# Output projection of a gated-attention layer: the first two token tiles interleaved, and the scaled rows kept in the weight rows' buffers

## The chip, the cores and the metric

The kernel runs on one core of a Trainium2 chip. The time is device microseconds (us) of one execution. TensorE (PE) multiplies matrices, VectorE (DVE), ScalarE (ACT) and GpSimd (POOL) work element by element, SyncE (SP) issues the DMAs. Every engine works through its own list of instructions in order and waits on semaphores.

## The reference, cut to what matters

One layer of a diffusion transformer, float32, 1024 tokens of width 1024. A gated linear attention `o_gla` (4 heads of 128) and a short row convolution `o_sc` (512 channels) stand side by side, and go through the output projection `w_out`:

```
o_gla = rmsnorm(o_f + o_b, g_head).reshape(bsz, t, GLA_WIDTH) * jax.nn.silu(og)
o_sc  = sb * dwconv_row(sc * sx, w_sc, b_sc, rows, width)
yx    = concatenate([o_gla, o_sc], axis=-1)
x     = x + gt1 * rmsnorm(yx @ w_out[i], g_post_mix[i])
hx    = modulate(rmsnorm(x, g_pre_ffn[i]), sh2, sc2)
x     = x + gt2 * rmsnorm(conv_ffn(hx, ...), g_post_ffn[i])
```

In the sum `yx @ w_out` the rows 512 to 1023 of `w_out` meet `o_sc`, which needs no gate any more (the *ungated half*); the rows 0 to 511 meet `o_gla`, which is first multiplied by `silu(og)` (the *gated half*).

## The kernel before

A float32 product is made of three matmuls (`mm3`, L144 to L146): each operand is split into a high part and a rest (`split`: ACT makes the high part at L127, DVE the rest at L134), and high x high, high x rest and rest x high are added in one PSUM bank. Tokens are tiled by 128, so there are 8 token tiles c = 0 to 7.

The order on PE is that in which the code is written. On ACT, DVE, POOL and SP a scheduler sets the order at build time, until token tile 7; from there on ACT, DVE and POOL keep the written order too, and SP alone is scheduled.

Names. `pw` is a memory pool that holds the first weight rows' split (`woh`, `wol` without number) and three buffers with the tag `wor` for raw rows of `w_out`; it is closed after the projection, and the pool `pc` of the next stage takes its place (raw rows `wr` of the up-projection, `u`, `rs`). `wp` holds `wraw`, `whi`, `wlo` in two buffers each. `ps_mm` has 4 PSUM banks. `scd` and `ogd` are spilled in DRAM: the convolution's results and the gate's arguments.

Tile c of the projection goes through these helpers (cut):

```
worder = (4, 5, 6, 7, 0, 1, 2, 3)

def mix_prep(c):                         # operands of tile c
    mh, ml = wp.tile(... "whi"), wp.tile(... "wlo")
    SY.dma_start(so, sc_d[c // 4][c % 4])
    split(so, mh[:, 4:8, :], ml[:, 4:8, :])          # ungated half
    SY.dma_start(sog, og_d[c // 4][c % 4])           # sog: 2 buffers
    SY.dma_start(xt, ap["x"][c * P : (c + 1) * P, :])
    PE.transpose(pt[...], on[c][...], ident)  x4     # L1031
    act(sf, sf, AF.Silu)                             # sf is sog
    V.scalar_tensor_tensor(sf, pt, col("ghead"), sf, ALU.mult, ALU.mult)   # L1034
    split(sog, mh[:, 0:4, :], ml[:, 0:4, :])         # gated half
def w_out(mh, ml, py, nhs, ns):          # mm3 per n in ns and half nh, contraction tile worder[n]
def half_stats(py, nh, xn, ss):          # ACT: sum of squares of a bank; DVE: xn = bank * gv1
def residual(c, xt, xn, ss, fill):       # POOL: rstd; DVE L1056: xt += xn * r; SP: x1_d[c] <- xt;
                                         # ACT: squares of xt into xn; POOL: rstd; DVE L1067: xn = xt * r
def norm_tiles():                        # L1075
    return p2.tile([P, D], F32, tag="xn", bufs=1, ...), cp.tile([P, 2], F32, tag="ss2", bufs=2, ...)
def norm2(c, xn, dg):                    # PE: 8 transposes of xn (L1086); ACT: 8 rows blk <- ps
```

So of the eight contraction steps n of a tile, n = 0 to 3 are ungated and n = 4 to 7 gated. A tile is 48 matmuls (8 steps, 2 halves of the output, 3 matmuls each). The loop calls `w_out` for tile 0 with n 0 to 3 of both halves, `mix_prep(1)`, then n 4 to 7, then `half_stats` of both halves and `residual`. For tiles 1 to 6: half 0 with all n, `mix_prep(c + 1)`, half 1 with n 0 to 4, `norm2(c - 1)`, `half_stats` of half 0, n 5 to 7, `half_stats` of half 1, `residual`. Tile 7 has its own order, in which the first up-projections are prepared too (`early_prep(p)`: a raw row `wr` is loaded, L1131, and split, L127 and L1181; tiles `p`). After the projection `early_dot(0)` to `early_dot(3)` and the products with the sums `mx` of `blk` follow on PE. The sums of weight rows `rs` (POOL, L1155) come from `wr` too.

Of the kernel before, what the change touches and what calls it, by code (L numbers as in the profile page):

```python
# [8 lines left out]
F32 = mybir.dt.float32  # L9
# [10 lines left out]
D = 1024  # L20
CT = 256
P = 128
KT = D // P
NT = T // P
# [94 lines left out]
def build(nc, ap, out, dbg=None):  # L119
# [3 lines left out]
    def nm(s="t"):  # L123
        return f"{s}{next(names)}"

    def act(o, i, fn=AF.Copy, **kw):
        return S.activation(o, i, fn, **kw)  # L127

    def split(raw, hi, lo, eng=None, heng=None):
        if heng is None:  # L130
            act(hi, raw)
        else:
            heng.tensor_copy(hi, raw)
        (eng or V).tensor_tensor(lo, raw, hi.bitcast(F32), ALU.subtract)  # L134
# [13 lines left out]
    with tile.TileContext(nc) as tc, tc.manual_schedule(engines={mybir.EngineType.PE}):  # L148
        pools = {}

        def popen(name, side=None, **kw):
            cm = tc.tile_pool(name=name, side=side, **kw)
            pools[name] = (cm, cm.__enter__())
            return pools[name][1]
# [9 lines left out]
        cp = popen("cp", "left", bufs=1)  # L164
# [4 lines left out]
        ps_mm, ps_at, ps_ms = "mm", "at", "ms"  # L169
# [4 lines left out]
        def bank(n):  # L174
            return pools[n][1].tile([P, 512], F32, tag=n, name=nm("ps"))
# [7 lines left out]
        def col(name, j=0, n=1):  # L183
            o, w = COLS[name]
            return cols[:, o + j : o + j + n]
# [806 lines left out]
        p2 = popen("p2", "right", bufs=1, reuse_waits="tile")  # L992
# [26 lines left out]
        def mix_prep(c):  # L1019
            mh = wp.tile([P, KT, P], F32R, tag="whi", name=nm("mh"))  # L1020
            ml = wp.tile([P, KT, P], F32R, tag="wlo", name=nm("ml"))
            so = pvo.tile([P, H, P], F32, tag="vo", name=nm("so"))
            SY.dma_start(so, sc_d[c // 4][c % 4])
            split(so, mh[:, 4:8, :], ml[:, 4:8, :])
            sog = p2.tile([P, H, P], F32, tag="sog", bufs=2, name=nm("sog"))
            SY.dma_start(sog, og_d[c // 4][c % 4])
            xt = p2.tile([P, D], F32, tag="x", bufs=2, name=nm("x"))
            SY.dma_start(xt, ap["x"][c * P : (c + 1) * P, :])
            pt = bank(ps_ms)
            for h in range(H):  # L1030
                PE.transpose(pt[:, h * P : (h + 1) * P], on[c][:, h * DV : (h + 1) * DV], ident)  # L1031
            sf = sog.rearrange("p h t -> p (h t)")
            act(sf, sf, AF.Silu)
            V.scalar_tensor_tensor(sf, pt, col("ghead"), sf, ALU.mult, ALU.mult)  # L1034
            split(sog, mh[:, 0:4, :], ml[:, 0:4, :])
            return mh, ml, xt

        def w_out(mh, ml, py, nhs, ns):
            for n in ns:
                kt = worder[n]  # L1040
                for nh in nhs:
                    s = slice(nh * 512, nh * 512 + 512)
                    mm3(py[nh], (mh[:, kt, :], ml[:, kt, :]), (woh[kt][:, s], wol[kt][:, s]), n == 0, n == KT - 1)

        def half_stats(py, nh, xn, ss):
            s = slice(nh * 512, nh * 512 + 512)
            act(xn[:, s], py[nh], AF.Square, scale=1.0 / 32, accum_out=ss[:, nh : nh + 1])
            V.tensor_tensor(xn[:, s], py[nh], gv1[:, s], ALU.mult)

        def residual(c, xt, xn, ss, fill):  # L1050
            r = cp.tile([P, 4], F32, tag="rstd", bufs=6, name=nm("rstd"))
            G.tensor_scalar(r[:, 0:1], ss[:, 0:1], ss[:, 1:2], EPS, ALU.add, ALU.add)
            G.tensor_tensor(r[:, 0:1], r[:, 0:1], mhalf[:, 0:1], ALU.pow)
            for f in fill[:1]:
                f()
            V.scalar_tensor_tensor(xt, xn, r[:, 0:1], xt, ALU.mult, ALU.add)  # L1056
            SY.dma_start(x1_d[c], xt)
            dump(f"x1_{c}", xt, [P, D])
            ss = cp.tile([P, 1], F32, tag="ss", bufs=4, name=nm("ss"))
            act(xn, xt, AF.Square, accum_out=ss)  # L1060
            r = rstd(ss, 1, 1.0 / D)
            for f in fill[1:3]:
                f()
            if c < NT - 1:
                for f in fill[3:]:
                    f()
                V.tensor_scalar(xn, xt, r[:, 0:1], None, ALU.mult)  # L1067
                return xn, None
            dg = p2.tile([P, P], F32, name="dg2")
            V.tensor_scalar(dg, ident, r[:, 0:1], None, ALU.mult)  # L1070
            for f in fill[3:]:
                f()
            return xt, dg

        def norm_tiles():  # L1075
            return p2.tile([P, D], F32, tag="xn", bufs=1, name=nm("xn")), cp.tile([P, 2], F32, tag="ss2", bufs=2, name=nm("ss2"))

        def norm2(c, xn, dg):
            cs = slice((c % 4) * P, (c % 4 + 1) * P)
            th = c // 4  # L1080
            for g in range(2):
                pt = bank(ps_at)
                for j in range(4):
                    o, i = pt[:, j * P : (j + 1) * P], xn[:, (4 * g + j) * P : (4 * g + j + 1) * P]
                    if dg is None:
                        PE.transpose(o, i, ident)  # L1086
                    else:
                        PE.matmul(o, i, dg, start=True, stop=True)
                for j in range(4):
                    ft = 4 * g + j  # L1090
                    act(blk[g][th][:, j, cs], pt[:, j * P : (j + 1) * P], AF.Identity,
                        bias=sh2[:, ft : ft + 1], scale=a2[:, ft : ft + 1])
            x11, x12, x21, x22 = (blk[g][h][:, :, cs] for g in range(2) for h in range(2))
            if th == 0:
                split(x11, b11[0][:, :, cs], b11[1][:, :, cs], heng=V)
                split(x21, b21[0][:, :, cs], b21[1][:, :, cs])
            else:
                d = t7[:, :, cs]
                return [lambda: V.tensor_tensor(d, x22, x12, ALU.subtract),
                        lambda: V.tensor_tensor(x12, x12, x11, ALU.subtract),  # L1100
                        lambda: V.tensor_tensor(x11, x11, d, ALU.add),
                        lambda: V.tensor_tensor(x21, x21, x11, ALU.subtract)]
# [81 lines left out]

        c2, c6, c1 = slice(0, 2 * P), slice(2 * P, 3 * P), slice(3 * P, 4 * P)
        gv1 = p2.tile([P, D], F32, name="gv1")
        mix = mix_prep(0)
        SY.dma_start(gv1, rows(16, "gp1"))
        gv2_row = rows(40, "gp2")
        normed = None  # L1190
        for c in range(NT):
            py = [bank(ps_mm) for _ in range(2)]
            mh, ml, xt = mix
            last, sums = normed, []
            if c == NT - 1:
                ordered = tc.manual_schedule(
                    engines={mybir.EngineType.Activation, mybir.EngineType.DVE, mybir.EngineType.Pool})
                ordered.__enter__()
            if c == 0:
                w_out(mh, ml, py, (0, 1), range(4))  # L1200
                mix = mix_prep(1)
                w_out(mh, ml, py, (0, 1), range(4, 8))
                xn, ss = norm_tiles()
                half_stats(py, 0, xn, ss)
            elif c == NT - 1:
                w_out(mh, ml, py, (0, 1), range(5))
                early_prep(0)()
                sums = norm2(c - 1, *last)
                mixed(6, c2)
                mixed(7, c2)  # L1210
                w_out(mh, ml, py, (0, 1), range(5, 6))
                w_out(mh, ml, py, (0,), range(6, 8))
                xn, ss = norm_tiles()
                half_stats(py, 0, xn, ss)
                w_out(mh, ml, py, (1,), range(6, 8))
            else:
                w_out(mh, ml, py, (0,), range(8))
                mix = mix_prep(c + 1)
                w_out(mh, ml, py, (1,), range(5))
                sums = norm2(c - 1, *last) or []  # L1220
                xn, ss = norm_tiles()
                half_stats(py, 0, xn, ss)
                w_out(mh, ml, py, (1,), range(5, 8))
            half_stats(py, 1, xn, ss)
            if c == NT - 1:
                sums.insert(1, early_prep(1))
            normed = residual(c, xt, xn, ss, sums)
# [156 lines left out]
        py = popen("py", "left", bufs=1)  # L1384
# [239 lines left out]
```

## Time and profile before

| what | value |
|---|---|
| median of 3 runs | 1183.76 us (1183.09 to 1184.44) |
| the profiled execution | 1187.9 us, of which the span from the first to the last instruction is 1186.1 us |
| mean granted clock of TensorE | 0.988 of full speed |
| busy share: PE, DVE, ACT, POOL | 97%, 74%, 44%, 40% |
| the output projection on PE | 427 to 533 us of the span |

PE is busy nearly throughout, so what matters are the places where it waits or runs at a lower clock. The table of PE's waits, the timeline of each engine, and the table of windows (with the granted clock) tell these.

### The profile page before, as it was taken

What the parts mean: (1) busy time and instruction counts of PE and PEld (TensorE: products, weight loads), DVE (VectorE), ACT (ScalarE), POOL (GpSimd) and SP (SyncE); (2) the same over time, 40 slices, a digit from 0 to 9 for tenths busy, and PEclk for the clock granted to TensorE, in tenths of its full rate; (3) what the DMA queues carried; (4) which work ended last, traced back from release to release, by engine and by line L of the source; (5) the groups of instructions that cost most, each with busy time, mean ns of one, the idle gap of its engine ahead of it and who ended that gap; (6) DMA issues with size and microseconds to landing.
All of it is one profiled execution on the core that took longest, in us unless ns stands there. A gap on an engine that the chain in (4) does not pass through costs nothing. (4 is left out here: it accounts for less than half of the span.)

```text
span 1186.1 us, 15908 instructions
## 1 busy us (share of the span) xinstructions
PE 1150.9 (97%) x5770; PEld 946.1 (80%) x5770; DVE 878.3 (74%) x1215; ACT 518.5 (44%) x931; POOL 479.0 (40%) x467
## 2 busy tenths in 40 slices
PE   8899999999999979999999999999999999999997
PEld 6689967877887868888787788888888888888885
DVE  4965547898769445559688987878787887777676
ACT  5745155643234145556343333333434254544453
POOL 3111001334355201114877776877686871000002
PEclk9999999999999989999999999999999999999999
DMA  9884854311102163232233442233223259978672
GB/s 347 269 293 136 266 153 134 121 57 46 54 18 75 60 217 129 107 125 71 76 101 100 134 141 71 90 125 116 85 79 125 95 161 326 361 246 278 215 241 98
DMA packets 80128, 176.19 MB, mean 149 GB/s; under 512 B 9809, under 2 KB 21585, under 8 KB 80050
## 3 DMA queue, kind: packets, MB, share of 16 engines
q1 hardware_dynamic: 80050, 175.19, 44.4%
q8 instruction: 45, 0.74, 0.3%
q14 instruction: 33, 0.27, 0.1%
HBM read 142.38 MB, written 32.78 MB: 148 GB/s over the span
## 5 line engine op out<-in xcount | busy, mean ns | idle before, releaser
L1296 DVE SCALAR_TENSOR_TENSOR y<-u,cols,y 128x945 f32<-128x945 f32 (+2 forms) x176 | 214.8, 1222 | 3.7 <-ACT y L127 1.3
L144 PE MATMUL ps<-mx,p 128*128 128x512 f32 x440 | 173.6, 395 | 2.9 <-ACT p L127 1.7
L145 PE MATMUL ps<-mx,p 128*128 128x512 f32 x440 | 173.0, 393 | 0.0
L146 PE MATMUL ps<-mx,p 128*128 128x512 f32 x440 | 172.7, 392 | 0.0
L134 POOL TENSOR_TENSOR p<-rs,p 128x512 fp32r<-128x512 f32 x88 | 116.3, 1326 | 88.8 <-ACT p L127 85.0
L146 PE MATMUL ps<-p,p 128*128 128x512 f32 x308 | 120.1, 390 | 0.2
L145 PE MATMUL ps<-p,p 128*128 128x512 f32 x308 | 120.0, 389 | 0.0
L144 PE MATMUL ps<-p,p 128*128 128x512 f32 x308 | 119.9, 389 | 0.0
L634 POOL TENSOR_TENSOR wl<-wr,wh 128x256 fp32r<-128x256 f32 x64 | 52.7, 854 | 159.3 <-ACT wh L127 159.2
L144 PE MATMUL ps<-hxh,wh 128*128 128x512 f32 x256 | 107.5, 420 | 0.0
L229 DVE CUSTOM_DVE_ANT_0 ada<-ada,cb 128x1024 f32<-128x1024 f32 x64 | 79.9, 1263 | 34.2 <-DMA ada<-in_ada 34.1
L144 PEld LDWEIGHTS ps<-mx,p 128*128 128x128 f32 x440 | 82.6, 188 | 25.8 <-ACT u L127 5.0
L146 PE MATMUL ps<-hxh,wl 128*128 128x512 f32 x256 | 101.4, 396 | 0.0
L145 PE MATMUL ps<-hxl,wh 128*128 128x512 f32 x256 | 101.0, 394 | 0.0
L146 PEld LDWEIGHTS ps<-mx,p 128*128 128x128 f32 x440 | 82.6, 188 | 18.6
L127 ACT ACTIVATE p<-rs 128x512 fp32r<-128x512 f32 x88 | 54.5, 622 | 98.0 <-POOL rs L1155 98.0
L145 PEld LDWEIGHTS ps<-mx,p 128*128 128x128 f32 x440 | 82.6, 188 | 18.3
L134 POOL TENSOR_TENSOR p<-wr,p 128x512 fp32r<-128x512 f32 x58 | 76.2, 1314 | 13.1 <-ACT p L127 13.1
L127 ACT ACTIVATE y<-u,cols 128x1024 f32<-128x1024 f32 x22 | 26.6, 1210 | 106.1 <-DVE u L1358 106.1
L144 PE MATMUL ps<-b,p 128*128 128x512 f32 x176 | 69.6, 396 | 0.0
L145 PE MATMUL ps<-b,p 128*128 128x512 f32 x176 | 69.4, 395 | 0.0
L146 PE MATMUL ps<-b,p 128*128 128x512 f32 x176 | 69.4, 394 | 0.0
(271 smaller groups left out, 2636.0 us busy)
## 6 DMA issues: line engine op xcount, KB each, us to landing
ada<-in_ada SPq DMA_DIRECT2D x64, 512.0 KB, 4.6
wr<-in_wu SPq DMA_DIRECT2D x48, 512.0 KB, 4.0
h<-hd SPq DMA_DIRECT2D x77, 256.0 KB, 4.3
hd<-h SPq DMA_DIRECT2D x73, 256.0 KB, 2.1
wdr<-in_wd SPq DMA_DIRECT2D x55, 256.0 KB, 4.0
wdr<-in_wd SPq DMA_DIRECT2D x22, 512.0 KB, 6.1
x<-in_x SPq DMA_DIRECT2D x16, 512.0 KB, 5.5
wr<-in_wb SPq DMA_DIRECT2D x16, 512.0 KB, 3.7
```

What stands on the lines that cost most here:

```text
L127: return S.activation(o, i, fn, **kw)
L134: (eng or V).tensor_tensor(lo, raw, hi.bitcast(F32), ALU.subtract)
L144: PE.matmul(ps, lh, rh, start=first, stop=False, skip_group_check=more)
L145: PE.matmul(ps, lh, rl, start=False, stop=False, skip_group_check=more)
L146: PE.matmul(ps, ll, rh, start=False, stop=last, skip_group_check=more)
L229: V.tensor_tensor_reduce(raw, raw, cbs[which], 1.0, 0.0, ALU.mult, ALU.add, dst)
L634: eng.tensor_tensor(lo[:, k : k + 2], raw[:, k : k + 2], hi[:, k : k + 2].bitcast(F32), ALU.subtract)
L1296: V.scalar_tensor_tensor(y3[:, ro, co], u3[:, ri, ci], col("wcf", 9 * p + 3 * (dr_ + 1) + dc + 1), y3[:, ro, co], ALU.mult, ALU.add)
```

## The change

Tiles 0 and 1 are prepared together ahead of the loop. PE works through the ungated half of tile 0, the ungated half of tile 1, the gated half of tile 0, the gated half of tile 1, in all four banks of `ps_mm`. `norm2(0)` moves from tile 1 to tile 2, behind 18 matmuls of its first half. In tiles 2 to 6 `half_stats` of half 0 is called ahead of `mix_prep(c + 1)`, instead of behind `norm2(c - 1)`. The scaled rows `xn` no longer have one buffer of their own in `p2`: they take the three `wor` buffers of `pw`. No operation is added or removed.

```
@@ norm_tiles
-            return p2.tile([P, D], F32, tag="xn", bufs=1, name=nm("xn")), cp.tile(...)
+            return pools["pw"][1].tile([P, D], F32, tag="wor", bufs=3, name=nm("xn")), cp.tile(...)
@@ before the loop
-        mix = mix_prep(0)
+        firsts = [mix_prep(0), mix_prep(1)]
         SY.dma_start(gv1, rows(16, "gp1"))
         gv2_row = rows(40, "gp2")
-        normed = None
-        for c in range(NT):
+        pys = [[bank(ps_mm) for _ in range(2)] for c in range(2)]
+        for c in range(2):
+            w_out(*firsts[c][:2], pys[c], (0, 1), range(4))
+        for c in range(2):
+            w_out(*firsts[c][:2], pys[c], (0, 1), range(4, 8))
+            xn, ss = norm_tiles()
+            for nh in range(2):
+                half_stats(pys[c], nh, xn, ss)
+            if c == 0:
+                mix = mix_prep(2)
+            firsts[c] = residual(c, firsts[c][2], xn, ss, [])
+        normed = firsts[1]
+        for c in range(2, NT):
@@ in the loop
-            if c == 0:
-                w_out(mh, ml, py, (0, 1), range(4))
-                mix = mix_prep(1)
-                w_out(mh, ml, py, (0, 1), range(4, 8))
-                xn, ss = norm_tiles()
-                half_stats(py, 0, xn, ss)
@@ tiles up to 6
-                w_out(mh, ml, py, (0,), range(8))
+                w_out(mh, ml, py, (0,), range(6))
+                if c == 2:
+                    norm2(0, *firsts[0])
+                w_out(mh, ml, py, (0,), range(6, 8))
+                xn, ss = norm_tiles()
+                half_stats(py, 0, xn, ss)
                 mix = mix_prep(c + 1)
                 w_out(mh, ml, py, (1,), range(5))
                 sums = norm2(c - 1, *last) or []
-                xn, ss = norm_tiles()
-                half_stats(py, 0, xn, ss)
                 w_out(mh, ml, py, (1,), range(5, 8))
```

What the scheduler makes of it stands in the order of the instructions. The first place is the start of the projection. On PE, before, at the end of tile 0's ungated half (`ps_3985` and `ps_3986` are tile 0's banks, `on` the attention output of the tile, `woh_3932` the first weight row of the gated half):

```order
L144 MATMUL ps_3986<-woh_3926,mh_3955 128x512
L145 MATMUL ps_3986<-wol_3927,mh_3955 128x512
L146 MATMUL ps_3986<-woh_3926,ml_3956 128x512
L1031 MATMUL ps_4021<-ident,on_3046 128x128 x4
L144 MATMUL ps_3985<-woh_3932,mh_3955 128x512
L145 MATMUL ps_3985<-wol_3933,mh_3955 128x512
L146 MATMUL ps_3985<-woh_3932,ml_3956 128x512
```

And with the change at the same point (tile 0 has the banks `ps_4004` and `ps_4005` now, tile 1 `ps_4006` and `ps_4007`):

```order
L144 MATMUL ps_4005<-woh_3926,mh_3955 128x512
L145 MATMUL ps_4005<-wol_3927,mh_3955 128x512
L146 MATMUL ps_4005<-woh_3926,ml_3956 128x512
L144 MATMUL ps_4006<-woh,mh_3974 128x512
L145 MATMUL ps_4006<-wol,mh_3974 128x512
L146 MATMUL ps_4006<-woh,ml_3975 128x512
```

The four transposes of tile 1 have gone ahead of all of this, and 24 matmuls of tile 1 stand between the ungated and the gated half of tile 0. On ACT, at the same place, before (`so` are the ungated operands, `sog` the gated ones; `mh_3955` is tile 0's operand, `mh_4011` tile 1's):

```order
L127 ACTIVATE mh_4011<-so_4013 128x512
L127 ACTIVATE woh_3948<-wor_3950 128x1024
L127 ACT_TABLE_LOAD
L127 ACTIVATE sog_3961<-sog_3961 128x512
L127 ACTIVATE mh_3955<-sog_3961 128x512
L127 ACTIVATE sog_4017<-sog_4017 128x512
L127 ACTIVATE mh_4011<-sog_4017 128x512
```

With the change:

```order
L127 ACTIVATE mh_3974<-so_3976 128x512
L127 ACTIVATE woh_3948<-wor_3950 128x1024
L127 ACT_TABLE_LOAD
L127 ACTIVATE sog_3961<-sog_3961 128x512
L127 ACTIVATE sog_3980<-sog_3980 128x512
L127 ACTIVATE mh_3955<-sog_3961 128x512
L127 ACTIVATE mh_3974<-sog_3980 128x512
```

The silu of tile 1 (`sog_3980`) has moved ahead of the high part of tile 0's gated operand.

The second place is SP's list of loads for the start of the projection. Before:

```order
L1023 DMA so_4099<-scd_1666 128x512
L1131 DMA wr_4753<-in_wu 128x1024
L1026 DMA sog_3961<-ogd_1664 128x512
L1028 DMA x_3963<-in_x 128x1024
L1188 DMA gv_3954<-row_3974 128x1024
L1026 DMA sog_4017<-ogd_1664 128x512
L1028 DMA x_4019<-in_x 128x1024
L1023 DMA so_4207<-scd_1666 128x512
```

With the change:

```order
L1023 DMA so_4088<-scd_1666 128x512
L1023 DMA so_4211<-scd_1666 128x512
L1131 DMA wr_4753<-in_wu 128x1024
L1026 DMA sog_3961<-ogd_1664 128x512
L1028 DMA x_3963<-in_x 128x1024
L1026 DMA sog_3980<-ogd_1664 128x512
L1028 DMA x_3982<-in_x 128x1024
L1189 DMA gv_3954<-row_3993 128x1024
```

The load of tile 3's ungated operand has moved from the end to ahead of both gated loads, and `gv` from between them to behind them.

The third place is SP at the end of the projection, where the raw weight rows of the next stage are loaded into `pc` (`wr_4933` and `wr_5019`, for `early_prep(2)` and `early_prep(3)`). Before:

```order
L1028 DMA x_4645<-in_x 128x1024
L1131 DMA wr_4933<-in_wu 128x1024
L1131 DMA wr_5019<-in_wu 128x1024
L1057 DMA x1d_1674<-x_4537 128x1024
L1131 DMA wr_5041<-in_wu 128x1024
L1057 DMA x1d_1675<-x_4645 128x1024
L1131 DMA wr_5042<-in_wu 128x1024
```

With the change:

```order
L1028 DMA x_4649<-in_x 128x1024
L1057 DMA x1d_1674<-x_4541 128x1024
L1131 DMA wr_5041<-in_wu 128x1024
L1057 DMA x1d_1675<-x_4649 128x1024
L1131 DMA wr_4933<-in_wu 128x1024
L1131 DMA wr_5019<-in_wu 128x1024
L1131 DMA wr_5042<-in_wu 128x1024
```

Both loads have moved behind the store of tile 7's rows. Ahead of `wr_4933` SP now waits for ACT as well, since `pc` lies where `pw` was, and the last user of `pw` is no longer a matmul of tile 7 but ACT's squares of tile 7's rows, which are written into `xn`.

More of the change, by code (lines that the diff above doesn't have):

```diff
@@ L1075, in norm_tiles @@
         def norm_tiles():
-            return p2.tile([P, D], F32, tag="xn", bufs=1, name=nm("xn")), cp.tile([P, 2], F32, tag="ss2", bufs=2, name=nm("ss2"))
+            return pools["pw"][1].tile([P, D], F32, tag="wor", bufs=3, name=nm("xn")), cp.tile([P, 2], F32, tag="ss2", bufs=2, name=nm("ss2"))
         def norm2(c, xn, dg):
@@ L1198, in build @@
                 ordered.__enter__()
-            if c == 0:
-                w_out(mh, ml, py, (0, 1), range(4))
-                mix = mix_prep(1)
-                w_out(mh, ml, py, (0, 1), range(4, 8))
-                xn, ss = norm_tiles()
-                half_stats(py, 0, xn, ss)
-            elif c == NT - 1:
+            if c == NT - 1:
                 w_out(mh, ml, py, (0, 1), range(5))
```

## The prediction

> **What bounds the kernel now.** I read the page's busy shares first, then the table of PE's waits, then the timeline of each engine around the two longest of these waits that the change touches.
>
> ```profile
> PE 1150.9 (97%) x5770; PEld 946.1 (80%) x5770; DVE 878.3 (74%) x1215; ACT 518.5 (44%) x931; POOL 479.0 (40%) x467
> ...
> PE ps L144 <- ACT mh L127: 6.5, 1, 6.5
> ...
> PE ps L144 <- ACT p L127: 1.7, 1, 1.7
> ...
> PE ps L1086 <- DVE xn L1067: 0.7, 1, 0.7
> ```
>
> PE sets the time: it is busy 97% of the span. Its longest wait of all is one wait of 6.5 us for `mh`, the high part of the projection's left operand. The waits of 1.7 and 0.7 us lie at the end of the projection and behind it. The reader is to see that only these three can be won or lost here; the number of matmuls stays the same. PE's timeline at the first of them:
>
> ```profile
> 426.71 0.60 PE L1031 MATMUL ps<-ident,on 128*128 128x128 f32 x4
> 427.07 0.48 PE L144 MATMUL ps<-woh,mh 128*128 128x512 f32 x1
> ...
> 432.63 0.60 PE L1031 MATMUL ps<-ident,on 128*128 128x128 f32 x4
> ...
> 439.76 0.80 PE L144 MATMUL ps<-woh,mh 128*128 128x512 f32 x1 [6.53 <-ACT mh L127]
> ...
> 443.43 0.39 PE L144 MATMUL ps<-woh,mh 128*128 128x512 f32 x1
> ```
>
> From 427.07 to 432.63 lie the 24 ungated matmuls of tile 0, 0.232 us each. Four transposes take 0.36 us (426.71 to 427.07), so the gated half could start at 432.99; it starts at 439.76, 6.77 us late. And from 439.76 to 443.43 only 9 matmuls start, in 3.67 us instead of 2.09: another 1.58 us. Why, the table of windows tells (time, then busy us and instructions of PE, PEld, DVE, ACT, POOL, granted clock, DMA share, GB/s):
>
> ```profile
> 435.00:436.00 1.00, 0.00 (x0) 0.00 (x0) 0.00 (x0) 0.00 (x0) 0.00 (x0) 1.00 1.13 379
> 436.00:437.00 1.00, 0.00 (x0) 0.00 (x0) 0.00 (x0) 0.67 (x1) 0.00 (x0) 0.61 0.91 318
> 437.00:438.00 1.00, 0.00 (x0) 0.00 (x0) 0.00 (x0) 0.99 (x2) 0.00 (x0) 0.50 1.05 424
> 442.00:443.00 1.00, 1.00 (x4) 0.76 (x3) 0.51 (x1) 0.00 (x0) 0.00 (x0) 0.50 0.89 334
> 443.00:444.00 1.00, 1.00 (x6) 0.83 (x5) 0.00 (x0) 0.52 (x1) 0.00 (x0) 0.97 0.93 301
> ```
>
> At 436.2 (0.61 of that microsecond), 3.0 us after PE fell idle at 433.23, the granted clock fell to one half, and it stayed there till 443. In all the place costs 6.77 + 1.58 = 8.35 us. Who is late there, ACT and DVE tell:
>
> ```profile
> 428.86 0.61 ACT L127 ACTIVATE mh<-so 128x512 fp32r<-128x512 f32 x1
> 430.13 0.69 DVE L134 TENSOR_TENSOR ml<-so,mh 128x512 fp32r<-128x512 f32 x1
> 436.33 1.28 ACT L127 ACT_TABLE_LOAD   x1 [4.00 <-DMA sog<-ogd]
> 437.63 0.63 ACT L127 ACTIVATE sog<-sog 128x512 f32<-128x512 f32 x1
> 438.29 0.75 DVE L1034 SCALAR_TENSOR_TENSOR sog<-ps,cols,sog 128x512 f32<-128x512 f32 x1 [4.71 <-ACT sog L127]
> 439.08 0.63 ACT L127 ACTIVATE mh<-sog 128x512 fp32r<-128x512 f32 x1 [0.82 <-DVE sog L1034]
> 439.74 0.69 DVE L134 TENSOR_TENSOR ml<-sog,mh 128x512 fp32r<-128x512 f32 x1 [0.69 <-ACT mh L127]
> ```
>
> The chain is: gate's arguments land (436.33), table load, silu, product, high part (done at 439.71). The ungated operands of tile 1 are long there: `mh` at 429.47, `ml` at 430.82.
>
> **The interleaving.** Eight transposes instead of four, then 48 ungated matmuls: PE starts them at 427.07 + 0.36 = 427.43 and has 48 x 0.232 = 11.12 us of work, to 438.55. Tile 1's operands (430.82) are wanted at 433.0, so nothing waits between. What is wanted at 438.55 is tile 0's gated operand. Two things move it: the queue of loads and ACT's order.
>
> ```profile
> 429.05 0.44 SPq L1026 DMA_DIRECT2D sog<-ogd  x1
> ...
> 430.48 0.71 SPq L1026 DMA_DIRECT2D sog<-ogd  x1
> ...
> DMA to landing us min/median/max: 9.2/9.2/9.2
> ```
>
> Tile 0's load, issued at 429.05, landed at 436.33; tile 1's, issued at 430.48, took 9.2 us, to 439.7. The DMAs are full (374 GB/s over the three windows from 435 to 438), so the order of the bytes decides. A further 256 KB load stands ahead of both now: 0.70 us, and tile 0's lands at 437.0. Between the two there is no `gv` any more, only `x` (512 KB): tile 1's lands 768 KB, 2.1 us, later, at 439.1 (at the latest as before, 439.7). Table load and silu take 436.33 to 438.29, 1.96 us: silu 0 ends at 439.0. ACT now does silu 1 next, which waits for 439.1 (439.7) and ends at 439.75 (440.35); then the high part, 0.65: PE can start at 440.4 (441.0). DVE makes both products (the second till 440.5, at the latest 441.1), then the rest part (0.7, till 441.2): the third matmul would be due 0.6 us behind the first, so it waits some 0.15 more. PE loses 1.85 to 2.45 plus 0.15; I take the middle, 2.3 us. The clock should stay full: PE was granted the full clock for 3.0 us of its idle time above.
>
> [...]
>
> So this place gives 8.35 - 2.3 = 6.05 us. Bounds: with both loads landing so early that only the old chain counts (439.76), 1.2 us are lost and 7.15 won; with the late landing 5.75.
>
> **What moves around it**, at nothing: `norm2(0)` stands 42 matmuls (9.7 us) behind tile 0's last matmul now, `norm2(1)` 39 and twelve transposes behind tile 1's. The chain between (squares, rstd, sum, squares, rstd, scaling) takes under 7.2 us, as tile 6 shows below; without those 2.5 us of cover each microsecond would be PE's. Silu 2 and 3 now stand ahead of tile 0's squares on ACT and may hold them for half a microsecond; the same cover takes it.
>
> **The squares of half 0 earlier, three buffers for `xn`.** Tile 6 is the one with a short cover:
>
> ```profile
> 520.97 0.64 ACT L127 ACTIVATE xn<-ps 128x512 f32<-128x512 f32 x1
> ...
> 521.54 0.64 ACT L127 ACTIVATE xn<-ps 128x512 f32<-128x512 f32 x1
> ...
> 528.17 1.09 PE L1086 MATMUL ps<-ident,xn 128*128 128x128 f32 x8 [0.68 <-DVE xn L1067]
> ```
>
> Both squares stand behind each other when PE is done. With the change the first is made long before, so the second starts at 520.97, 0.57 us sooner, and the chain to 528.17 with it. I take 0.55 of the 0.68 us (bounds 0 and 0.68). In tiles 2 to 5 PE doesn't wait here, so it is worth nothing there.
>
> **The price: raw rows later.** `wr_4933` and `wr_5019` were loaded at 522.08; now they wait for ACT's squares of tile 7.
>
> ```profile
> 522.08 0.82 SPq L1131 DMA_DIRECT2D wr<-in_wu  x2
> ...
> 538.81 0.18 ACT L127 ACTIVATION_READ_ACCUMULATOR xn<-x 128x1 f32 x1
> 539.04 0.33 SPq L1131 DMA_DIRECT2D wr<-in_wu  x1
> ...
> DMA to landing us min/median/max: 3.5/3.5/3.5
> ...
> 542.49 1.14 ACT L127 ACTIVATE p<-wr 128x512 fp32r<-128x512 f32 x2
> 542.96 1.47 POOL L1155 TENSOR_TENSOR rs<-wr,wr 128x512 f32<-128x512 f32 x1 [2.67 <-DVE mx L134]
> 543.20 3.48 DVE L1181 TENSOR_TENSOR p<-wr,p 128x512 fp32r<-128x512 f32 x2
> 544.51 1.62 POOL L1155 TENSOR_TENSOR rs<-wr,rs 128x512 f32<-128x512 f32 x1
> 546.60 0.68 DVE L1099 TENSOR_TENSOR t<-blk,blk 128x512 f32<-128x512 f32 x1
> 548.77 0.73 ACT L127 ACTIVATE mx<-blk 128x256 fp32r<-128x256 f32 x2 [2.35 <-DVE blk L1101]
> 566.71 0.67 DVE L1351 TENSOR_TENSOR g<-u,ps 128x512 f32<-128x512 f32 x1
> 567.53 0.47 PE L144 MATMUL ps<-mx,p 128*128 128x512 f32 x1 [1.72 <-ACT p L127]
> ```
>
> In before's times: the squares end at 538.99, `wr_4933` is issued where `wr_5042` was (539.04) and lands 3.5 us later, at 542.55; ACT wants it at 542.49. That is 0.06 us late: nothing. `wr_5042` comes third; at 1.4 us per 512 KB (374 GB/s) it lands 2.85 us later than before, at 545.4, and POOL's two sums `rs` with it. Their reader on ACT stands far behind, but POOL then works at 545.4 to 548.5, where DVE's chain L1099 to L1102 towards `mx` starts (546.60). While POOL ran its two sums before, two DVE rows took 3.48 us, not 2 x 0.68: each lasted as long as POOL's. So L1099 and L1100 are held instead, about 1 us net of what L1181 wins (it is alone now). That chain has no slack at the end: PE waits 1.72 us at 567.53, and DVE's reading of the bank it wants ends at 567.38. Between, ACT and DVE idle some tenths, which absorb a part. I take 0.6 us lost (bounds 0 and the whole 2.85).
>
> [...]
>
> **Sum.** 6.05 + 0.55 - 0.6 = 6.0 us. The profiled execution, 1187.9 us (span 1186.1), would be 1181.9 (1180.1). It lies 4.1 us above the median of the runs, 1183.76; taken off that, 1177.8 us.
>
> **Rivals.**
> *The clock falls again* (1180.4 us). If tile 1's gate lands later than 440.3, PE idles over 3.0 us: 3.05 + 0.15 lost and 1.58 for the half clock, 2.5 more than forecast. For it: 9.2 us for such a load now; against: less stands ahead of it than before.
> *The collision at the end is dear* (1179.1 to 1180.1 us). L1099 waits out both sums, from 546.6 to 548.5 (1.9 us), or the whole 2.85 us of POOL's delay reach 567.53. For it: the two rows of 3.48 us and no slack at 567.53; against: L1181 wins at the same time, and POOL's readers come late. [...]
> *Slower* (from 1186.2 us). ACT keeps `p<-wr_4933` ahead of tile 7's `blk` rows, so every microsecond by which the load lands behind 542.5 goes into the chain to 567.53. Without the collision 6.6 us are won, so 10.1 us from issue to landing eat it all, and 12.5 us make the kernel slower by 0.2%. The loads above took up to 9.2 us in a full queue; at 539 one took 3.5. A landing of 9.2 would give 1182.9.
> *Nothing changes* (1183.8 us). If tile 1's ungated operands are late and PE waits ahead of them instead. Against: ready at 430.82, wanted at 433.0.
>
> **How the numbers follow.** Forecast 0.64; clock 0.12; collision 0.12; nothing 0.04; a late landing short of slower 0.04; slower 0.04. Within 0.2% (2.4 us, about what a measurement of this kernel can tell) lie the fourth and fifth: 0.08; slower 0.04; faster 0.88. The range goes from 7.15 + 0.68 won (1175.9) to the two dearer rivals with a microsecond for their sizes (1181.4).
>
> **What would show it.** In the changed profile: PE's wait ahead of tile 0's gated half of 1.8 to 2.5 us instead of 6.53, at a clock of 1.00; one row of eight transposes at 426.7; the wait at L1086 in tile 7 down to 0.1; two `wr` loads at the store of tile 7's rows; the wait of 1.72 us grown to 2 to 3. Wrong it would be if PE idled at `early_dot(2)` or `norm2(0)`, or if the clock row showed 0.50 again.

## The result, and the profile after

The changed kernel takes 1177.94 us in the median (1176.24 to 1178.64, 5 runs), the kernel before on the same chip 1183.76 us (1182.38 to 1185.46, 5 runs): a ratio of 0.9944, 95% interval 0.9924 to 0.9963. On another chip it came to 0.9957 (0.9943 to 0.9971). So 5.8 us were won by the medians (their quotient is 0.9951; the interval of the ratio allows 4.4 to 9.0 us); forecast were 6.0. The sum came out nearly as forecast because two errors cancelled: the interleaving won more than was put down for it, and the end of the projection cost more, through a fall of the clock that had not been foreseen.

The profiled execution took 1176.24 us, span 1174.3. The page's first line of busy shares, and of the table of PE's waits the two that the change touches (engine, what waits, for what, us in total, times, longest):

```profile
PE 1146.1 (98%) x5770; PEld 941.0 (80%) x5770; DVE 880.5 (75%) x1215; ACT 518.3 (44%) x931; POOL 485.0 (41%) x467
```

```profile
PE ps L144 <- DVE g L1360: 2.2, 1, 2.2
...
PE ps L144 <- ACT mh L127: 0.6, 1, 0.6
```

The wait of 6.5 us for `mh` is down to 0.6, and the 0.7 us at L1086 is gone from the table. The wait of 1.7 us at the up-projection has become 2.2, and it ends with another operation: the bank that DVE frees, not ACT's operand. PE's timeline at these places:

```profile
420.63 1.03 PE L1031 MATMUL ps<-ident,on 128*128 128x128 f32 x8
...
433.20 0.50 PE L144 MATMUL ps<-woh,mh 128*128 128x512 f32 x1 [0.61 <-ACT mh L127]
...
514.32 1.09 PE L1086 MATMUL ps<-ident,xn 128*128 128x128 f32 x8
...
554.16 0.66 PE L144 MATMUL ps<-mx,p 128*128 128x512 f32 x1 [2.17 <-DVE g L1360]
554.62 0.63 PE L145 MATMUL ps<-mx,p 128*128 128x512 f32 x1
```

Eight transposes stand in one row; tile 7's transposes (514.32) have no bracket, so they did not wait. The last two rows show the unforeseen loss: 0.66 and 0.63 us for matmuls that take 0.39 elsewhere. The chain of the gate on SP and ACT:

```profile
423.59 0.40 SPq L1026 DMA_DIRECT2D sog<-ogd  x1
...
424.62 0.44 SPq L1026 DMA_DIRECT2D sog<-ogd  x1
```

```profile
429.77 1.28 ACT L127 ACT_TABLE_LOAD   x1 [3.78 <-DMA sog<-ogd]
431.07 1.24 ACT L127 ACTIVATE sog<-sog 128x512 f32<-128x512 f32 x2
432.52 1.29 ACT L127 ACTIVATE mh<-sog 128x512 fp32r<-128x512 f32 x2 [0.21 <-DVE sog L1034]
```

Silu 0 and 1 follow each other without a gap (x2, 1.24 us), so tile 1's load was not late. And DVE and POOL at the place of the forecast price, ahead of `mx`:

```profile
532.88 1.03 DVE L1099 TENSOR_TENSOR t<-blk,blk 128x512 f32<-128x512 f32 x1 [2.02 <-ACT blk L127]
533.95 1.67 DVE L1100 TENSOR_TENSOR blk<-blk,blk 128x512 f32<-128x512 f32 x1
```

```profile
532.08 1.29 POOL L1155 TENSOR_TENSOR rs<-wr,wr 128x512 f32<-128x512 f32 x1 [5.62 <-DMA wr<-in_wu]
533.45 1.62 POOL L1155 TENSOR_TENSOR rs<-wr,rs 128x512 f32<-128x512 f32 x1
```

POOL waits 5.62 us for the raw row that now comes late, and its sums lie on L1099 and L1100: 2.70 us for both, where they took 0.68 and 0.69. The row comes late because SP issues three of them together now, when ACT's squares of tile 7 have ended (525.15):

```profile
525.18 1.31 SPq L1131 DMA_DIRECT2D wr<-in_wu  x3
```

How this reaches PE's wait, a later sum of POOL tells. First before, then with the change, with ACT's row that waits for it:

```profile
561.59 1.29 POOL L1155 TENSOR_TENSOR rs<-wr,rs 128x512 f32<-128x512 f32 x1
...
562.07 4.12 DVE L134 TENSOR_TENSOR mx<-blk,mx 128x1024 fp32r<-128x1024 f32 x2 [0.98 <-ACT mx L127]
```

```profile
549.17 3.45 DVE L134 TENSOR_TENSOR mx<-blk,mx 128x1024 fp32r<-128x1024 f32 x2 [0.49 <-ACT mx L127]
...
549.21 2.34 POOL L1155 TENSOR_TENSOR rs<-wr,rs 128x512 f32<-128x512 f32 x1
...
551.58 0.63 ACT L127 ACTIVATE p<-rs 128x512 fp32r<-128x512 f32 x1 [1.50 <-POOL rs L1155]
```

Before, the sum starts 0.48 us ahead of DVE's two rows and takes 1.29 us. Now it starts 0.04 us behind them and takes 2.34. ACT waits 1.50 us for it and then reads a bank into `u`, DVE goes on with L1258 and L1360, and only then is PE's bank free.

Spans of single profiles can't be compared directly here: ahead of the projection both kernels have the same code, and yet it began at 426.71 us in the profile of before and at 419.9 to 424.1 in all others. So below I count **PE's way**: from the projection's first transposes to the end of PE's last matmul. Its pieces are the projection (to the first matmul `ps<-b,p`), the products of the first prefetched rows (to the first `ps<-mx,p`, 24.3 us, but 24.8 in e3_swap_loads and 24.4 in e8_grid_c), the stretch from there to the next `ps<-b,p`, in which PE waits for the bank or the operand, and the rest (604.8 to 605.0 us). All profiles of this study, in us:

| kernel | PE's way | projection | wait at the gated half | wait at `mx,p` | from `mx,p` to the next `b,p` |
|---|---|---|---|---|---|
| before | 751.38 | 106.50 | 6.53 | 1.72 | 15.68 |
| before_again | 751.32 | 106.51 | 5.43 | 1.73 | 15.71 |
| after | 745.69 | 98.74 | 0.61 | 2.17 | 17.72 |
| after_again | 746.39 | 99.68 | 1.57 | 2.02 | 17.59 |
| e6_grid_a (after) | 744.89 | 98.28 | 0.17 | 1.81 | 17.36 |
| e7_grid_b (after) | 743.78 | 98.60 | 0.46 | 2.01 | 15.97 |
| e1_own67 | 744.07 | 99.19 | 1.06 | 1.72 | 15.67 |
| e1_again | 743.90 | 99.07 | 0.94 | 1.75 | 15.71 |
| e2_bufs_only | 750.82 | 105.47 | 5.70 | 2.16 | 16.13 |
| e3_swap_loads | 745.47 | 99.58 | 1.42 | 2.11 | 16.11 |
| e8_grid_c (as e3) | 746.16 | 99.10 | 0.97 | 2.16 | 17.70 |
| e4_half_interleave | 750.00 | 104.74 | 4.62 | 2.07 | 16.06 |
| e5_late_raw | 742.40 | 97.55 | 0 | 1.74 | 15.69 |

### The profile page after: what moved, and what is told of

It reads as the page before. It is cut to its first block, busy times and chain, and to the rows that moved or that the text cites. A ratio compares the mean times of both kernels' runs of the same rounds, so it can differ in the third digit from the quotient of the medians.

```text
span 1174.3 us, 15910 instructions
## 1 busy us (share of the span) xinstructions
PE 1146.1 (98%) x5770; PEld 941.0 (80%) x5770; DVE 880.5 (75%) x1215; ACT 518.3 (44%) x931; POOL 485.0 (41%) x467
## 5 line engine op out<-in xcount | busy, mean ns | idle before, releaser
L634 POOL TENSOR_TENSOR wl<-wr,wh 128x256 fp32r<-128x256 f32 x64 | 57.9, 936 | 153.6 <-ACT wh L127 153.6
```

The lines of the kernel that those rows point to most:

```text
L634: eng.tensor_tensor(lo[:, k : k + 2], raw[:, k : k + 2], hi[:, k : k + 2].bitcast(F32), ALU.subtract)
```

## The experiments

**The price undone: tiles 6 and 7's scaled rows in a buffer of their own.** All else is the changed kernel; the raw rows no longer have to wait for tile 7's squares.

```
-        def norm_tiles():
-            return pools["pw"][1].tile([P, D], F32, tag="wor", bufs=3, ...), ...
+        def norm_tiles(c):
+            xn = p2.tile([P, D], F32, tag="xn", bufs=1, ...) if c >= NT - 2 \
+                 else pools["pw"][1].tile([P, D], F32, tag="wor", bufs=3, ...)
```

> The changed kernel, but the scaled rows of token tiles 6 and 7 take a buffer of their own in p2 again (tiles 0 to 5 stay in the wor buffers). The raw rows wr for the early products are then issued during tile 7's first matmuls, not behind ACT's squares of tile 7. As a measure I take PE's way from the projection's first transposes to PE's last matmul: 751.0 us in the profile of before, 745.3 in that of the changed kernel. Theory A (the buffers cost 2 us at the start of the up-projection, through GpSimd's sums that run later against VectorE's rows, and the clock that falls in the longer wait): PE's wait there is 1.7 us or less with the full clock, the way 743.2 to 743.8, the time about 1176.0. Rival B (the longer wait and the fallen clock are chance, or come from the earlier start, not from the buffers): wait 2.0 to 2.3, way 745 to 745.5, time 1177.9.

SP issues the two raw rows during tile 7 again, and PE waits for ACT's operand as before:

```profile
508.72 0.81 SPq L1132 DMA_DIRECT2D wr<-in_wu  x2
```

```profile
553.58 0.47 PE L144 MATMUL ps<-mx,p 128*128 128x512 f32 x1 [1.72 <-ACT p L127]
```

The wait is 1.72 us, as in before, and the stretch that holds it 15.67 (before 15.68). So the shared buffers, through the raw rows, make the whole of the longer wait. PE's way is 744.07 us, 0.3 above what was expected, because the wait at the gated half was 1.06 us here. Time: 1176.41 us in the median, ratio to before 0.9948 (0.9929 to 0.9967), 1175.20 and 0.9937 (0.9921 to 0.9952) when run again:

> The kernel of e1_own67 once more, beside e5_late_raw on the same chip. Both theories: first wait 0.6 to 1.4 us, up-projection's wait 1.7 us at full clock, PE's way 743.8 to 744.5; the time about 1.4 to 1.6 us under the changed kernel's if that kernel's clock falls as a rule in its 2.17 us wait, about 0.4 us under it if it seldom does.

There the changed kernel had 0.9957 on the same chip. The difference of 2.25 us between the two medians goes the way that PE's way says (743.9 against 743.8 to 746.4), but the intervals of the ratios overlap.

**The buffers alone.** Before, with only `norm_tiles` changed as in the change.

> The kernel before with one line changed: the scaled rows xn in the three wor buffers. No interleaving. Theory A: the first wait of 6.5 us at half clock stays, the wait in tile 7 (0.68 us) nearly goes, since two buffers let the squares of half 0 go ahead; the up-projection's first wait grows from 1.72 to 2.0 to 2.3 us and the clock may fall in it (1.6 us). Way 750.8 (clock full) to 752.5 (clock fallen), time 1183.6 to 1185.3. Rival B: way 750.4, wait 1.7, time 1183.2. Rival C (the buffers are what made the kernel faster): way under 748.

```profile
523.83 1.09 PE L1086 MATMUL ps<-ident,xn 128*128 128x128 f32 x8
```

The row has no bracket: tile 7's wait is gone without the earlier `half_stats`. With three buffers the squares of tile 6's half 0 no longer wait for the reader of the last `xn`, and the scheduler sets them early by itself. The wait at `mx,p` grows to 2.16 us. The two nearly cancel: PE's way is 0.5 us shorter, and the time is the same, ratio 0.9998 (0.9985 to 1.0010). So the buffers alone win nothing, and the 5.8 us come from the rest of the change. The earlier `half_stats` can add to that only where PE waits, in tile 7, and there the buffers alone remove the wait too; so nearly all of it is the interleaving.

**Half an interleaving.** Only the first two ungated steps of tile 1 stand ahead of tile 0's gated half: 12 matmuls instead of 24.

```
-            w_out(*firsts[c][:2], pys[c], (0, 1), range(4))
+            w_out(*firsts[c][:2], pys[c], (0, 1), range((4, 2)[c]))
```

> The changed kernel with only two of tile 1's four ungated steps ahead of tile 0's gated half: 12 matmuls (2.8 us) less of cover. Theory A (the gate's chain has a fixed end, PE's wait is what the cover leaves): PE's wait ahead of tile 0's gated half grows from 0.6 to 3.4 us. [...] Rival E (the wait shrank because the loads landed earlier, not because of the cover): wait under 2 us.

```profile
433.87 0.80 PE L144 MATMUL ps<-woh,mh 128*128 128x512 f32 x1 [4.62 <-ACT mh L127]
```

The rival, that the wait had shrunk because the loads landed earlier, is out: the wait came back. It is longer than expected, because this load was among the slowest (7.24 us; with the 6.2 us of the changed kernel's first profile it would be 3.6, an estimate), and the clock fell (0.50 from 431.85 to 438.67): PE's way is 750.0 us, the time 1179.94 us. The cover must reach to the end of the gate's chain; half of it gave less than a quarter of the gain (1.4 of some 6 us) in this one execution with its slow load.

**The loads in another order.** The pair's weight rows (`load_up(0)`) are asked for ahead of the third prefetched row, in the changed kernel.

```
+        load_up(0)
         early_prep(2)()
...
-        load_up(0)
```

> The changed kernel with the raw rows of the first full product (whose sums GpSimd makes) loaded ahead of those of the early products 2 and 3; the buffers stay as changed. Only the order of three loads differs. Theory A: GpSimd's sums start 2.5 to 3 us earlier, as in the kernel before, and the split of the early product's row 1.4 us later. If the collision of the sums with VectorE's chain is what grew the wait, it falls to 1.7 us or below; if the late split (rival D) is what counts, it grows to 2.5 to 3.5 us and the clock falls again. Way 743.5 by A, 746 or more by D.

The collision is gone, and another wait stands in its place:

```profile
535.20 0.69 DVE L1099 TENSOR_TENSOR t<-blk,blk 128x512 f32<-128x512 f32 x1 [1.34 <-ACT blk L127]
535.93 0.69 DVE L1100 TENSOR_TENSOR blk<-blk,blk 128x512 f32<-128x512 f32 x1
```

```profile
531.23 1.16 ACT L127 ACTIVATE p<-wr 128x512 fp32r<-128x512 f32 x2 [2.01 <-DMA wr<-in_wu]
```

ACT waits 2.01 us for the prefetched row now, with tile 7's `blk` rows queued behind it: this is the mechanism of the rival "Slower", in small. So DVE ends L1100 about as late as in the changed kernel, POOL's later sum takes 2.34 us again, and the wait at `mx,p` stays at 2.11 us: neither expectation came out. Another 0.5 us are lost ahead of it (0.15 in a second execution of this kernel, e8_grid_c; one time: 1175.87 us). Which of the late loads comes first makes no gain; all must be issued earlier, as in the first experiment.

**The load that stood ahead of the gates.** This is the first experiment, and in addition the first prefetched raw row, 512 KB that are not wanted until tile 7, stands behind the gates' loads.

```
-        SY.dma_start(gv1, rows(16, "gp1"))
+        after_gv = SY.dma_start(gv1, rows(16, "gp1"))
+        with tc.issue_after(after_gv.ins):       # SP keeps what follows behind gv1's load
+            first_raw = up_raw(0, True)
...
-            raw = up_raw(p, True)
+            raw = up_raw(p, True) if p else first_raw
```

> The changed kernel with tiles 6 and 7's scaled rows in their own buffer (as e1_own67), and in addition the first prefetched raw weight row (512 KB, L1132, for early_prep(0), not needed before tile 7) queued behind the loads of gates 0 and 1, of x 0 and 1 and of gv1, where it stood ahead of all of them on SP. Theory A (bytes ahead in the queue set when gate 0 lands, and gate 0 sets the first L144's wait): gate loads of 256 KB with 512 KB x loads between them landed 1.0 us (423.59 to 429.7 against 424.62 to 431.6: 1.9 to 2.0 us apart for 768 KB), so 512 KB less ahead lands gate 0 about 1.3 us sooner; the first wait of 1.06 us (e1_own67) goes to 0, PE's way from 744.07 to 743.0 (742.8 to 743.4), and the time is about 1.0 us under e1_own67's on the same chip. Theory B (gate 0 takes some 6 us from issue whatever stands ahead of it; the first wait is its latency): the wait stays 0.6 to 1.4 us, the way 743.6 to 744.5. Both: the wait at the up-projection stays 1.7 to 2.2 us.

SP's queue, ACT's table load, and PE from the first transposes on in one window (time, busy us and instructions of PE, PEld, DVE, ACT, POOL, granted clock, DMA share, GB/s), the latter with the changed kernel's behind it:

```profile
424.75 0.45 SPq L1026 DMA_DIRECT2D sog<-ogd  x1
...
427.66 0.60 SPq L1132 DMA_DIRECT2D wr<-in_wu  x1
```

```profile
430.08 1.28 ACT L127 ACT_TABLE_LOAD   x1 [2.30 <-DMA sog<-ogd]
```

```profile
422.43:440.28 17.85, 17.85 (x86) 14.94 (x85) 8.29 (x10) 9.47 (x15) 0.00 (x0) 1.00 0.85 300
```

```profile
420.63:438.48 17.85, 17.24 (x79) 13.78 (x78) 7.92 (x9) 8.37 (x12) 0.00 (x0) 1.00 0.89 299
```

PE is busy 17.85 of 17.85 us. The gate's arguments took 5.33 us to land instead of 6.66 and 6.71 in the two profiles of the first experiment: 1.3 us less for 512 KB less, as at 374 GB/s (1.4 us). But the same load took 5.84 to 7.27 us in the four profiles of the changed kernel, so one profile does not show that the 512 KB make the whole difference. With an issue that also came earlier they are there 7.65 us behind the first transposes, where the other kernels had 8.5 to 10.4. PE's way is 742.40 us, 1.5 to 1.7 us under that of the first experiment and 0.4 under the lowest value expected. The time, 1175.06 us in the median (1173.95 to 1176.51, ratio to before 0.9934, 0.9918 to 0.9951), is the lowest median of this study; from 1175.20 for the first experiment on the same chip it can't be told apart.

**Why the clock fell in a wait of 2 us.** In the changed kernel the clock was halved behind the wait of 2.17 us, though waits of 2.07, 2.11 and 2.16 us in other kernels left it full. The first step was to see whether that comes again, and whether the projection's late start in the profile of before does:

> The changed kernel once more. Its profile had the clock at 0.50 for some 3.5 us after a wait of 2.17 us at the up-projection (1.6 us of PE time), while waits of 2.07, 2.11 and 2.16 us in three other kernels left the clock full. Theory A (whether so short a wait is punished depends on where it falls against something that the program does not set): wait 2.1 to 2.2 us, clock full in this profile more likely than not (3 in 4), PE's way then 744.1 to 744.6. Rival B (this kernel's wait is punished as a rule, being the longest of the four): clock at 0.50 again, way 745.4 to 746.0. Both: first wait 0.5 to 1.5 us at full clock.

> The kernel before once more. Theory A (the 6 us by which its profiled execution began the projection later than all others, 426.7 against 420.0 to 423.4, belong to that execution and not to the kernel): projection begins at 420 to 424, span 1171.5 to 1175.5 plus 6 us of PE's longer way, so 1177 to 1183; rival B (the change reaches back to the work ahead of the projection): it begins at 426 to 427 again, span about 1186. Both: first wait 5.7 to 6.6 us, half clock after it, tile 7's wait 0.6 to 0.7, PE's way 750.9 to 751.8.

The clock fell again (0.50 from 556.74 to 560.15, a stretch of 17.59 us), so the rival was ahead; the way of 746.39 us lay above both ranges, since the wait at the gated half was 1.57 us. The projection of before began at 421.12 us, so the late start belonged to that one execution, and its way was the same, 751.32 us (its first wait, 5.43 us, was shorter than expected).

Then I read off every fall and rise of the clock in the ten profiles at hand. In each they lie on a grid of 3.413 us that runs through the whole execution, to 0.01 us, and each execution has another phase (its lines lie 0.36 to 2.85 us past a whole number of steps from the span's start). In the profile of after: falls at 161.74 and 554.28, 392.54 us apart, which are 115.0 steps. Windows cut on the grid show it, first early in the program, then at the wait:

```profile
158.33:161.74 3.41, 1.89 (x7) 0.74 (x5) 3.29 (x6) 1.93 (x3) 0.00 (x0) 1.00 0.00 0
161.74:165.16 3.42, 3.42 (x8) 2.72 (x9) 0.69 (x1) 0.67 (x3) 0.00 (x0) 0.50 0.12 12
```

```profile
550.86:554.27 3.41, 1.24 (x6) 0.73 (x6) 3.31 (x4) 2.64 (x5) 3.41 (x3) 1.00 0.47 130
554.27:557.68 3.41, 3.41 (x9) 2.64 (x10) 0.94 (x2) 0.00 (x0) 3.33 (x4) 0.50 0.62 183
557.68:561.10 3.42, 3.42 (x16) 2.79 (x15) 0.69 (x1) 0.63 (x1) 3.42 (x3) 1.00 0.00 0
```

The clock is exactly 1.00 or 0.50 in each. (The first of these windows was followed by a fall although it had 1.89 us of work; what is said below of the bound holds for the later rows only.) The wait lies wholly in the window from 550.86, which has 1.24 us of PE work in 3.41; the next one runs at half clock, with 9 matmuls instead of 16. In the kernel with the loads in another order the grid cuts a wait of the same length in two (2.39 and 2.33 us of work), and the clock stays full:

```profile
550.64:554.05 3.41, 2.39 (x11) 1.66 (x9) 3.31 (x3) 1.91 (x4) 3.41 (x2) 1.00 0.15 28
554.05:557.47 3.42, 2.33 (x10) 1.97 (x11) 2.14 (x4) 1.15 (x3) 3.42 (x4) 1.00 0.82 243
```

So the theory was: what counts is not the length of the wait but how much of it falls into one window. Three more executions tested it, at the phase that each happened to have (the stretch in the expectations is the last column of the table above, the wait included):

> The changed kernel, as a test of a grid. Over the ten profiles so far every fall and rise of the granted clock lies within 0.01 us on a grid of 3.413 us that runs through a whole execution, with another phase in each; a window of the grid with 1.24 or 1.39 us of PE work was followed by one window at half clock, one with 1.67 to 2.00 us (projection and up-projection) was not. Theory A (grid): read the phase from the falls near 32, 160 and 260 us; the wait of 2.0 to 2.2 us at the up-projection is followed by one window of 3.41 us at 0.50 exactly if one window of that grid holds more than 1.75 to 2.02 us of it; the chance of that is 0.43 to 0.59; with the fall the stretch from the wait's end to the next product is 17.4 to 17.8 us, without it 15.9 to 16.2. Rival B (this kernel's wait is always followed by a fall): 17.4 to 17.8 us whatever the phase.

> The changed kernel once more; as e6_grid_a, with the phase that this execution happens to have. Theory A: fall exactly if one window of the grid holds more than 1.75 to 2.02 us of the wait. Rival B: fall whatever the phase.

> The kernel of e3_swap_loads (weight loads of the pair ahead of the third prefetch), whose wait of 2.11 us left the clock full. Theory A (grid): there the wait lay across a boundary (1.02 and 1.09 us on either side); at another phase, with more than 1.75 to 2.02 us in one window, the clock falls in this kernel too, and the stretch to the next product is 17.4 to 17.8 us; else 15.9 to 16.2. Rival B (this order of loads protects it): full clock whatever the phase. Both: wait 2.0 to 2.2 us, first product to the up-projection's 24.7 to 24.9 us.

Of the first, the window with the wait and the one behind it; of the second, the two that share the wait; of the third, as of the first:

```profile
550.65:554.06 3.41, 1.60 (x8) 1.26 (x8) 2.87 (x5) 1.98 (x4) 3.41 (x3) 1.00 0.67 203
554.06:557.48 3.42, 3.42 (x10) 2.65 (x9) 0.69 (x1) 0.18 (x1) 3.34 (x4) 0.50 0.28 109
```

```profile
549.69:553.10 3.41, 2.42 (x11) 1.68 (x9) 3.31 (x3) 1.92 (x5) 3.41 (x2) 1.00 0.21 34
553.10:556.51 3.41, 2.39 (x11) 2.01 (x12) 2.07 (x4) 1.08 (x3) 3.41 (x4) 1.00 0.70 246
```

```profile
555.65:559.07 3.42, 1.26 (x6) 0.86 (x5) 3.32 (x5) 2.50 (x5) 3.42 (x3) 1.00 0.61 176
559.07:562.48 3.41, 3.41 (x9) 2.67 (x8) 0.07 (x1) 0.00 (x0) 3.33 (x3) 0.50 0.40 136
```

The same kernel falls in the first (a wait of 1.81 us in one window) and not in the second (2.01 us, cut into 0.99 and 1.02). The kernel with the loads in another order, full before, falls in the third. Both rivals are refuted. The second and the third decide this: the first wait was shorter than expected (1.81 us instead of 2.0 to 2.2) and fell into the range that the theory had left open (1.75 to 2.02), so it only narrows the bound. (For the third, 24.7 to 24.9 us had been expected for the first products; they took 24.4.) The bound is narrow: 1.60 us of work in a window (1.81 idle) halves the next; 1.68 in e5_late_raw (1.74 idle) does not:

```profile
551.03:554.45 3.42, 1.68 (x8) 1.09 (x7) 3.42 (x4) 1.64 (x3) 3.42 (x3) 1.00 0.71 224
554.45:557.86 3.41, 3.41 (x16) 2.80 (x17) 1.46 (x3) 0.00 (x0) 3.33 (x3) 1.00 0.17 67
```

The waits of 1.72 to 1.75 us (before, and the kernels with tile 6 and 7's own buffer) were never followed by a fall; of the eight of 1.81 to 2.17 us in the table four were, as the grid cut them. The single times of the three executions are 1174.68, 1174.62 and 1180.35 us; the last had three windows at half clock ahead of the projection already, the others one each.

## Why the prediction was right

**The interleaving: mechanism right, the wait taken too long.** Forecast were 6.05 us won, with 2.3 lost in a wait at the gated half. The four profiles of the changed kernel wait 0.61, 1.57, 0.17 and 0.46 us, at full clock. The bracket is not the whole loss: in the first of them the last ungated matmul starts at 432.20 and the gated one was due 0.23 later, so 0.77 are lost, and up to the fourth gated matmul (434.27) another 0.38 are lost, most of it around the third, which waits for `ml`: 1.15 in all (forecast 0.15 for that matmul). The projection takes 98.3 to 99.7 us instead of 106.5, 7.7 less in the mean; without the 0.7 of tile 7 that is 7.0 us, close to the forecast's own bound of 7.15. The chain from the landing to PE's first gated matmul was right: 3.42 or 3.43 us in every profile that waited, forecast 3.4. What was mis-sized is the landing. I had added 0.7 us to the one landing that the profile of before showed (436.33, 9.62 us behind the first transposes). But the load took long in that execution (7.28 us from its issue to the table load behind it; 6.20 in the second profile of before), and in the changed kernel's profiles it took 5.84 to 7.27 us. The slowest of them, 10.10 us behind the first transposes, comes near the 10.3 that I had forecast, and its wait of 1.57 near the lower end of 1.85. For tile 1's load I had the spacing nearly right (2.1 us; it is 1.94 to 1.97), but it does not count: table load and silu 0 fill that time.

**Tile 7: size right, cause half wrong.** The wait of 0.68 us is gone, as forecast (0.55 of it). I had put that down to the earlier square of half 0; the buffers alone do it too.

**The price: right in mechanism.** The raw rows land late, POOL's sums lie on L1099 and L1100, DVE loses 1.33 us there (2.70 less 1.37), and the wait at `mx,p` grows by 0.45, 0.30, 0.09 and 0.29 us, forecast 0.6. Counted from the moment at which PE falls idle there, L1100 ends 1.45, 1.30, 1.09 and 1.29 us later than in before: the wait grows by 1.0 us less each time, and so it does in the four profiles of other kernels with late raw rows (1.35 to 1.45 us later, the wait 0.35 to 0.44 longer). So 1.0 us was slack, where the prediction had counted 0.4. In all eight POOL's later sum takes 2.34 or 2.35 us and PE's matmul starts 2.61 or 2.62 us behind its end; in the five profiles without late rows the sum takes 1.29 or 1.30 and PE does not wait for it. L1099 and L1100 end 0.54 and 0.55 us behind POOL's two sums, where alone each takes 0.68 or 0.69, so they were held nearly to the end of them. The 1.9 us of the dear rival, L1099 waiting out both sums, were too high for PE because of that slack.

**The step that failed: "the clock should stay full".** I had concluded from 3.0 us of full clock in one wait that waits of 2 us are free. The 3.0 us said only where the grid stood at that time: the window from 432.81 to 436.23 held the idle time (0.42 us of PE work), and the fall came at its end. A window that was idle in part was enough in e6_grid_a, 1.81 of 3.41 us (53%). So that conclusion is the step that was wrong, at the end of the projection instead of its start: in three of the four profiles of the changed kernel the fall took 1.6 us (9 matmuls instead of 16 in a window, 7 x 0.227). My rival of a second fall looked at the gated half, and there it did not come; but a clock row of 0.50 was named as a sign of being wrong, and it did appear, at the other place.

**The sum.** In the mean of the four profiles: 7.0 won by the interleaving (forecast 6.05), 0.7 in tile 7 (0.55), 0.3 lost by the longer wait (0.6) and 1.2 by the clock (nothing): 6.2 us of PE's way, forecast 6.0. So the right sum is in part luck: the interleaving was put 0.95 us too low, the end of the projection 0.9 us too cheap, the clock included. To take 4.1 us off for the profiled execution of before fits what its second profile shows; a likely reason is below. One rival is added up slightly wrong: by its own terms the second fall of the clock gives 1180.2 to 1180.3 us, not 1180.4.

## What to carry to other kernels

Where an operand comes late, work that does not need it belongs ahead of it up to the end of its whole chain, and loads that nobody wants yet belong behind it in the queue (with 512 KB moved there PE's way was 1.5 to 1.7 us shorter, in one profile); half a cover gave less than a quarter of the gain, in one execution. A buffer that is shared to gain freedom at one place takes it at another: ask which load waits for its last reader. Between these rows of 128x512 matmuls a wait costs its length and, from about 1.8 us on, with some chance (four of eight here) another 1.6 us of half clock; pulling it below that bound can win more than the time by which it is shortened (from after to e1_own67 the wait lost 0.45 us, the stretch that holds it 2.05).

## What had not been expected of the hardware

- The clock's grid of 3.413 us has the same step in all 13 profiles, at phases from 0.14 to 2.85 us (e3_swap_loads and e6_grid_a lie 0.01 apart). PE's way of the changed kernel was 743.78 us where the grid cut the wait, and 744.89 to 746.39 in the three profiles with the fall. Of two falls at the gated half, before and before_again, one came 3.0 us into the wait and one 4.4; the waits were 6.53 and 5.43 us, and in the second more of the half clock fell on matmuls (5.75 us against 3.29), which made the projections equal (106.50 and 106.51 us).
- The time ahead of the projection differs too, perhaps by the phase. Profiles with one window at half clock there began the projection at 419.87 and 420.91 us, that of before, with five, at 426.71. This fits the spread of the times between runs of one kernel (1178.9 to 1186.2 us for before on one chip); it was not tried by itself, and the number of such windows alone does not order the starts (with three of them 421.12, 422.43 and 424.08 us).
- The bound holds for these rows of 128x512 matmuls. Early in the program windows with 1.50 to 2.32 us of PE work were followed now by a full and now by a half clock; what else counts there stays open.
